# Log-softmax over 50,000 columns: the loads move from SyncE's queue to GpSimd's

## The chip, the cores and the metric

The kernel runs on one core of a Trainium2 chip. The core has five engines that run their own instruction streams and wait for one another through semaphores: TensorE (PE in the profile), VectorE (DVE), ScalarE (ACT), GpSimd (POOL) and SyncE (SP). Sixteen DMA engines move data between the chip's large memory (HBM) and the core's on-chip memory (SBUF, 128 partitions). A DMA is issued by an instruction of one of the engines. The metric is the device time of one execution in microseconds, the median of several runs.

## What is computed

For each of 16 x 512 = 8192 rows of 50,000 float32 values, the logarithm of the softmax:

```python
def reference(x: np.ndarray) -> np.ndarray:       # x: (16, 512, 50000)
    max_x = np.max(x, axis=-1, keepdims=True)
    shifted = x - max_x
    log_sum_exp = np.log(np.sum(np.exp(shifted), axis=-1, keepdims=True))
    return (shifted - log_sum_exp).astype(np.float32)
```

The input is 1638.4 MB, the output as much. Each value is read once and written once by the kernel.

## The kernel before

A tile is 32 rows, each cut in four quarters, so that 128 partitions hold 12,500 values each: 50,000 B per partition, 6.4 MB per tile, 256 tiles. Four buffers of that size fill SBUF. A tile lives in one buffer from its load to its store: it is loaded, reduced, exponentiated into a throw-away place for the sum, corrected in place, and stored from there.

Each engine has a part of its own; semaphores join them. `landed[j]` tells that the load into buffer j has landed, `stored[j]` that its store is done. A DMA adds 16 to its semaphore when it is complete. `take` waits for 16 and takes them off again, so that the same constant serves in each round.

```python
def take(engine, sem, n=16):
    engine.wait_ge(sem, n).then_inc(sem, -n)

@block.gpsimd
def _(gpsimd):
    view = ones.rearrange("p (r g) -> p r g", g=G)
    gpsimd.memset(ones, 1.0).then_inc(ready)
    # ... two affine_selects leave 1.0 where two partitions belong to one row

@block.sync
def _(sync):
    def load(j, src):
        sync.dma_start(out=bufs[j], in_=src).then_inc(landed[j], 16)

    for t in range(NBUF):
        load(t, xt[t])
    src = run(xt, NBUF, rounds)
    with sync.Fori(0, rounds) as q:           # 63 rounds of four tiles
        for j in range(NBUF):
            take(sync, stored[j])
            load(j, src(q, j))
    # ... then waits for the last stores
```

VectorE waits for the landing, takes the maxima of the four column pieces, spreads the row's maximum over its four partitions with two small transposes, and, once ScalarE and TensorE have made the logarithm of the sum, subtracts both in place:

```python
    def whole(j, by_pieces=False):
        take(vector, landed[j])
        for c in range(NS):                   # NS = 4 pieces of 3125 columns
            vector.tensor_reduce(
                out=negms[j][:, c : c + 1], in_=bufs[j][:, cols(c)],
                op=ALU.max, axis=AX, negate=True,
            ).then_inc(...)
        # ... negp, share(j), scaled
        subtract(j, ...)                      # tensor_scalar on the whole 128 x 12500 buffer

    with vector.Fori(0, rounds):
        for j in range(NBUF):
            whole(j)
        settle()
    for j in range(NBUF):
        whole(j, by_pieces=j == NBUF - 1)
```

ScalarE exponentiates piece by piece, with the sum as a by-product, and issues the stores. The store of a tile is issued in the midst of the next tile's work, ahead of its third piece (`GATE = 2`):

```python
        for c in range(NS):
            if c == GATE and dst is not None:
                store((j - 1) % NBUF, dst, bufs[(j - 1) % NBUF])
            shifted.next(scalar.activation(out=dump, in_=bufs[j][:, cols(c)], func=ACT.Exp, ...))
```

TensorE adds up the four partitions of a row with a matrix of ones (the one that GpSimd makes at the start).

Of the kernel before, what the change touches and what calls it, by code (L numbers as in the profile page):

```python
# [19 lines left out]
NBUF = 4  # L20

NS = 4
# [22 lines left out]
def take(engine, sem, n=16):  # L45

    engine.wait_ge(sem, n).then_inc(sem, -n)  # L47


def cols(c):  # L50
    return slice(c * C, (c + 1) * C)
# [3 lines left out]
def kernel(  # L55
# [14 lines left out]
    rounds = (ntiles - NBUF) // NBUF  # L70
    assert ntiles % NBUF == 0 and rounds >= 2

    xt = xf.rearrange("(t r) (g w) -> t (r g) w", r=R, g=G)
    ot = of.rearrange("(t r) (g w) -> t (r g) w", r=R, g=G)

    def run(a, first, n):

        part = a[first : first + NBUF * n].rearrange("(q i) p w -> q i p w", i=NBUF)
        return lambda q, i: part[bass.ds(q, 1), i].rearrange("o p w -> (o p) w")
# [13 lines left out]
    bufs = [data.tile([P, W], FP32, name=f"buf{j}") for j in range(NBUF)]  # L93
# [19 lines left out]
    def sem(name):  # L113
        return ctx.enter_context(nc.semaphore(name))

    landed = [sem(f"landed{j}") for j in range(NBUF)]
    stored = [sem(f"stored{j}") for j in range(NBUF)]
# [11 lines left out]
    block = ctx.enter_context(nc.Block())  # L129

    @block.gpsimd
    def _(gpsimd):
        view = ones.rearrange("p (r g) -> p r g", g=G)
        gpsimd.memset(ones, 1.0).then_inc(ready)  # L134
        gpsimd.affine_select(  # L135
            out=view, in_=view, pattern=[[-G, R], [0, G]], base=0,
            channel_multiplier=1, compare_op=ALU.is_ge, fill=0.0,
        ).wait_op(ready, 1, "sem-ge").then_inc(ready)
        gpsimd.affine_select(  # L139
            out=view, in_=view, pattern=[[G, R], [0, G]], base=G - 1,  # L140
            channel_multiplier=-1, compare_op=ALU.is_ge, fill=0.0,
        ).wait_op(ready, 2, "sem-ge").then_inc(ready)

    @block.sync
    def _(sync):
        def load(j, src):
            sync.dma_start(out=bufs[j], in_=src).then_inc(landed[j], 16)

        for t in range(NBUF):
            load(t, xt[t])  # L150
        src = run(xt, NBUF, rounds)
        with sync.Fori(0, rounds) as q:
            for j in range(NBUF):
                take(sync, stored[j])
                load(j, src(q, j))
        for j in range(NBUF - 1):
            take(sync, stored[j])
        take(sync, stored[NBUF - 1], 16 * NS)

    @block.vector  # L160
    def _(vector):
        def share(k):

            on_dve.next(
                vector.transpose(out=allneg, in_=negp.to_broadcast([P, SQ]))  # L165
            ).then_inc(on_dve.sem)
            on_dve.next(
                vector.tensor_reduce(  # L168
                    out=rowneg, in_=allneg.rearrange("p (r g) -> p r g", g=G),
                    op=ALU.min, axis=AX,  # L170
                )
            ).then_inc(on_dve.sem)
            on_dve.next(
                vector.tensor_copy(  # L174
                    out=spread.rearrange("p (r g) -> p r g", g=G),
                    in_=rowneg[:, :, None].to_broadcast([P, SQ // G, G]),
                )
            ).then_inc(on_dve.sem)
            on_dve.next(
                vector.transpose(out=negmaxs[k], in_=spread)  # L180
            ).then_inc(agreed.sem)

        def subtract(k, *bufs):
            for n, buf in enumerate(bufs):
                ins = vector.tensor_scalar(  # L185
                    out=buf, in0=buf, scalar1=negmaxs[k][:, 0:1], scalar2=logs[k],
                    op0=ALU.add, op1=ALU.subtract,
                )
                if n == 0:
                    logged.next(ins)  # L190
                ins.then_inc(subtracted.sem)

        def whole(j, by_pieces=False):
            take(vector, landed[j])

            for c in range(NS):
                vector.tensor_reduce(  # L197
                    out=negms[j][:, c : c + 1], in_=bufs[j][:, cols(c)],
                    op=ALU.max, axis=AX, negate=True,
                ).then_inc(shifted.sem if c < NS - 1 else on_dve.sem)  # L200
            on_dve.next(vector.nop()).then_inc(shifted.sem)  # L201
            vector.tensor_reduce(  # L202
                out=negp, in_=negms[j], op=ALU.min, axis=AX
            ).then_inc(on_dve.sem)
            share(j)

            rescaled.next(
                vector.tensor_mul(out=scaleds[j], in0=scales[j], in1=parts[j])  # L208
            ).then_inc(summed.sem)
            subtract(j, *([bufs[j][:, cols(c)] for c in range(NS)] if by_pieces else [bufs[j]]))  # L210

        def settle():
            for count in (on_dve, rescaled, logged):
                count.settle(vector)

        with vector.Fori(0, rounds):
            for j in range(NBUF):
                whole(j)
            settle()
        for j in range(NBUF):  # L220
            whole(j, by_pieces=j == NBUF - 1)

    @block.scalar
    def _(scalar):
# [97 lines left out]
```

## Time and profile before

| | before |
|---|---|
| time, median of 3 runs | 7589.62 us (7589.4 to 7590.59) |
| span of the profiled execution | 7588.4 us |
| tiles | 256, so 29.6 us each |
| VectorE waits for landings, in total | 923.3 us in 251 waits, the longest 18.9 |
| a load's issue on SyncE's queue | 333 ns median, 256 of them |
| a store's issue on ScalarE's queue | 339 ns median, 259 of them |
| first reduction on VectorE begins | 18.94 us |

The profile records one execution. Busy times say how much each engine worked; a row of 40 digits shows the busy share in tenths for 40 equal slices of the span; the waits say which engine sat idle for which other one. Moving data is no engine's busy time: it has a row of its own, with the mean busy share of the sixteen DMA engines and the bytes that they moved. An issue of a DMA is short; the time from issue to landing is listed apart. SPq, ACTq and DVEq stand for the engines' instruction queues, where waits and DMA issues are handled.

### The profile page before, as it was taken

How to read it: one execution, taken by the hardware profiler on the slowest of the kernel's cores; microseconds unless marked ns; L12 is line 12 of the kernel's file. 1: busy time of each engine (PE TensorE's matmuls, PEld its weight loads, DVE VectorE, ACT ScalarE, POOL GpSimd, SP SyncE). 2: the span in 40 equal slices, each digit the busy share in tenths (PEclk: the TensorE clock that was granted, in tenths of full speed). 3: DMA queues.
4: the chain of work that ended last, by engine and by line, in shares of the span. 5: the costliest groups of instructions: out<-in, count | busy, mean ns of one | idle time of the engine just before them, and what ended most of it. 6: DMA issues, size and time to landing. Idle time of an engine off the chain costs nothing. (4 is left out here: it accounts for less than half of the span.)

```text
span 7588.4 us, 13821 instructions
## 1 busy us (share of the span) xinstructions
PE 477.9 (6%) x2048; PEld 456.0 (6%) x2048; DVE 5440.6 (72%) x2819; ACT 3184.7 (42%) x2561; POOL 1.4 (0%) x7
## 2 busy tenths in 40 slices
PE   0000000000000000000000000000000000000000
PEld 0000000000000000000000000000000000000000
DVE  7767677777777777777777777777777777777776
ACT  4434444344443434444344443434444344444433
POOL 0000000000000000000000000000000000000000
DMA  9999999999999999999999999999999999999999
GB/s 417 432 432 433 434 431 434 434 433 433 434 433 431 434 434 433 431 434 433 432 434 434 431 434 434 432 433 434 434 431 434 434 434 432 434 434 431 434 434 400
DMA packets 74162, 3276.85 MB, mean 432 GB/s; under 512 B 8240, under 2 KB 8240, under 8 KB 8240
## 3 DMA queue, kind: packets, MB, share of 16 engines
q1 hardware_dynamic: 36864, 1638.42, 50.0%
q10 hardware_dynamic: 37296, 1638.42, 50.0%
q14 instruction: 2, 0.02, 0.0%
HBM read 1638.40 MB, written 1638.40 MB: 432 GB/s over the span
## 5 line engine op out<-in xcount | busy, mean ns | idle before, releaser
L239 ACT ACTIVATE dump<-buf,negm 128x3125 f32<-128x3125 f32 x1024 | 2937.3, 2868 | 3805.0 <-DVE negm L197 3765.7
L197 DVE TENSOR_REDUCE negm<-buf 128x1 f32<-128x3125 f32 x1024 | 3418.2, 3400 | 923.3 <-DVEq L47 923.3
L185 DVE TENSOR_SCALAR buf<-buf,negmax,logsum 128x12500 f32<-128x12500 f32 (+1 forms) x259 | 1738.9, 6715 | 553.8 <-ACT logsum L227 553.8
L277 PE MATMUL sums<-scaled,ones 128*128 128x1 f32 x2048 | 477.9, 355 | 7087.2 <-DVE scaled L208 7087.2
L277 PEld LDWEIGHTS sums<-scaled,ones 128*128 128x128 f32 x2048 | 456.0, 328 | 7109.0 <-DVE scaled L208 7109.0
L208 DVE TENSOR_TENSOR scaled<-scale,part 128x4 f32<-128x4 f32 x256 | 41.6, 163 | 580.4 <-ACT scale L247 580.4
L227 ACT ACTIVATE logsum<-sums 128x1 f32<-128x1 f32 x256 | 43.8, 171 | 551.0 <-PE sums L277 551.0
L239 ACT ACTIVATION_READ_ACCUMULATOR dump<-buf,negm 128x1 f32 x1024 | 190.8, 186 | 0.0
L247 ACT ACTIVATE scale<-negm,negmax 128x4 f32<-128x4 f32 x256 | 76.1, 297 | 23.6
L202 DVE TENSOR_REDUCE negp<-negm 128x1 f32<-128x4 f32 x256 | 40.1, 157 | 39.2 <-DVE negm L197 39.2
L180 DVE STREAM_TRANSPOSE negmax<-spread 128x32 f32<-128x32 f32 x256 | 54.2, 212 | 8.9
L165 DVE STREAM_TRANSPOSE allneg<-negp 128x32 f32<-128x32 f32 x256 | 54.1, 211 | 8.9
L168 DVE TENSOR_REDUCE rowneg<-allneg 128x8 f32<-128x32 f32 x256 | 47.6, 186 | 8.9
L174 DVE COPY spread<-rowneg 128x32 f32<-128x32 f32 x256 | 46.3, 181 | 8.9
L258 ACT ACT_TABLE_LOAD x1 | 1.3, 1283 | 1.0 <-SPq L111 1.0
L135 POOL TENSOR_SCALAR_AFFINE_SELECT ones<-ones 128x128 f32<-128x128 f32 x1 | 0.5, 519 | 0.1
L139 POOL TENSOR_SCALAR_AFFINE_SELECT ones<-ones 128x128 f32<-128x128 f32 x1 | 0.5, 519 | 0.1
L134 POOL MEMSET ones<- 128x128 f32 x1 | 0.2, 205 | 0.5 <-SPq L111 0.5
L306 POOL MEMSET const-bfloat16-1.0<- 128x1 bf16 x1 | 0.1, 103 | 0.0
L306 POOL MEMSET const-uint8-127<- 128x1 uint8 x1 | 0.1, 102 | 0.0
L306 POOL MEMSET const-float32-0.0<- 128x1 f32 x1 | 0.1, 99 | 0.3 <-issue 0.3
L306 POOL MEMSET const-float32-1.0<- 128x1 f32 x1 | 0.1, 99 | 0.0
## 6 DMA issues: line engine op xcount, KB each, us to landing
buf<-in_x_dram SPq DMA_DIRECT2D x256, 6250.0 KB, 36.7
out_dram<-buf ACTq DMA_DIRECT2D x255, 6250.0 KB, 41.6
out_dram<-buf ACTq DMA_DIRECT2D x4, 1562.5 KB, 11.3
```

Of the source, the lines that this page charges most:

```text
L165: vector.transpose(out=allneg, in_=negp.to_broadcast([P, SQ]))
L168: vector.tensor_reduce(out=rowneg, in_=allneg.rearrange("p (r g) -> p r g", g=G), op=ALU.min, axis=AX,)
L174: vector.tensor_copy(out=spread.rearrange("p (r g) -> p r g", g=G), in_=rowneg[:, :, None].to_broadcast([P, SQ // G, G]),)
L180: vector.transpose(out=negmaxs[k], in_=spread)
L185: ins = vector.tensor_scalar(out=buf, in0=buf, scalar1=negmaxs[k][:, 0:1], scalar2=logs[k], op0=ALU.add, op1=ALU.subtract,)
L197: vector.tensor_reduce(out=negms[j][:, c : c + 1], in_=bufs[j][:, cols(c)], op=ALU.max, axis=AX, negate=True,).then_inc(shifted.sem if c < ...
L202: vector.tensor_reduce(out=negp, in_=negms[j], op=ALU.min, axis=AX).then_inc(on_dve.sem)
L208: vector.tensor_mul(out=scaleds[j], in0=scales[j], in1=parts[j])
L227: scalar.activation(out=logs[k], in_=rowsums[k], func=ACT.Ln)
L239: scalar.activation(out=dump, in_=bufs[j][:, cols(c)], func=ACT.Exp, bias=negms[j][:, c : c + 1], scale=1.0, accum_out=parts[j][:, c : c + 1],
L247: scalar.activation(out=scales[j], in_=negms[j], func=ACT.Exp, bias=negmaxs[j][:, 0:1], scale=-1.0,)
L277: ins = tensor.matmul(rowsums[j], ones, scaleds[j][:, c : c + 1], start=c == 0, stop=c == NS - 1,)
```

## The change

The loads are issued by GpSimd instead of SyncE. A DMA issued by SyncE or ScalarE has its descriptors (the records that tell a DMA engine what to move) made by hardware; one issued by GpSimd has them made by software on that engine. SyncE is left with nothing to do. GpSimd first issues the four loads of the start, then makes the matrix of ones, then goes through the loop of waits and loads.

VectorE no longer takes 16 off `landed[j]` after each landing. The count grows: in round q it waits for 16(q + 1), a value that is computed from the loop's counter into a register once a round, and for the last four tiles for a constant.

```diff
@@ GpSimd and SyncE @@
     @block.gpsimd
     def _(gpsimd):
         view = ones.rearrange("p (r g) -> p r g", g=G)
+
+        def load(j, src):
+            gpsimd.dma_start(out=bufs[j], in_=src).then_inc(landed[j], 16)
+
+        for t in range(NBUF):
+            load(t, xt[t])
         gpsimd.memset(ones, 1.0).then_inc(ready)
 # ... (the two affine_selects as they were)
-
-    @block.sync
-    def _(sync):
-        def load(j, src):
-            sync.dma_start(out=bufs[j], in_=src).then_inc(landed[j], 16)
-
-        for t in range(NBUF):
-            load(t, xt[t])
         src = run(xt, NBUF, rounds)
-        with sync.Fori(0, rounds) as q:
+        with gpsimd.Fori(0, rounds) as q:
             for j in range(NBUF):
-                take(sync, stored[j])
+                take(gpsimd, stored[j])
                 load(j, src(q, j))
         for j in range(NBUF - 1):
-            take(sync, stored[j])
-        take(sync, stored[NBUF - 1], 16 * NS)
+            take(gpsimd, stored[j])
+        take(gpsimd, stored[NBUF - 1], 16 * NS)
@@ VectorE @@
-        def whole(j, by_pieces=False):
-            take(vector, landed[j])
+        def whole(j, nth, by_pieces=False):
+            vector.wait_ge(landed[j], nth)
 # ...
-        with vector.Fori(0, rounds):
+        with vector.Fori(0, rounds) as q:
+            nth = vector.snap(q * 16 + 16)
             for j in range(NBUF):
-                whole(j)
+                whole(j, nth)
             settle()
         for j in range(NBUF):
-            whole(j, by_pieces=j == NBUF - 1)
+            whole(j, 16 * (rounds + 1), by_pieces=j == NBUF - 1)
```

The order of the computing instructions on VectorE, ScalarE and TensorE is the same as before.

## The prediction

> **What bounds the kernel now.** I read the page first: its shares of busy time, its DMA row in 40 slices, and its list of DMA issues.
>
> ```profile
> span 7588.4 us, 13821 instructions
> PE 477.9 (6%) x2048; PEld 456.0 (6%) x2048; DVE 5440.6 (72%) x2819; ACT 3184.7 (42%) x2561; POOL 1.4 (0%) x7
> ...
> DMA  9999999999999999999999999999999999999999
> ...
> HBM read 1638.40 MB, written 1638.40 MB: 432 GB/s over the span
> ...
> buf<-in_x_dram SPq DMA_DIRECT2D x256, 6250.0 KB, 36.7
> out_dram<-buf ACTq DMA_DIRECT2D x255, 6250.0 KB, 41.6
> ```
>
> No compute engine is near full; the DMA engines are, in every slice. The stretches in windows say whether that is really a ceiling (the last two columns are the DMA share and GB/s):
>
> ```profile
> 500.00:1000.00 500.00, 29.87 (x128) 28.50 (x128) 356.58 (x186) 209.12 (x167) 0.00 (x0) 1.00 1.00 433
> 2000.00:4000.00 2000.00, 126.94 (x544) 121.12 (x544) 1435.73 (x747) 839.62 (x676) 0.00 (x0) 1.00 1.00 433
> 7530.00:7590.00 60.00, 3.74 (x16) 3.56 (x16) 29.75 (x22) 15.90 (x14) 0.00 (x0) 1.00 0.75 319
> ```
>
> In the middle the share is 1.00 at a flat 433 GB/s. All 3276.8 MB at 433 GB/s take 7568 us; only some 20 us of 7588 are start and tail, most of it in the last 60 us, where the share is 0.75. So the time is bytes over rate, and only four things can move it: the rate, gaps in which both DMA queues are empty, the start, the tail.
>
> Next, how far each queue is from running empty. The timeline of two tiles in the middle:
>
> ```profile
> 3004.72 0.34 ACTq L231 DMA_DIRECT2D out_dram<-buf  x1
> ...
> 3013.98 6.79 DVE L185 TENSOR_SCALAR buf<-buf,negmax,logsum 128x12500 f32<-128x12500 f32 x1 [2.16 <-ACT logsum L227]
> 3017.01 29.84 SPq L147 DMA_DIRECT2D buf<-in_x_dram  x2
> 3024.32 13.35 DVE L197 TENSOR_REDUCE negm<-buf 128x1 f32<-128x3125 f32 x4 [3.55 <-DVEq L47]
> ...
> 3034.24 0.34 ACTq L231 DMA_DIRECT2D out_dram<-buf  x1
> ...
> 3043.50 6.79 DVE L185 TENSOR_SCALAR buf<-buf,negmax,logsum 128x12500 f32<-128x12500 f32 x1 [2.16 <-ACT logsum L227]
> 3053.82 13.35 DVE L197 TENSOR_REDUCE negm<-buf 128x1 f32<-128x3125 f32 x4 [3.53 <-DVEq L47]
> ```
>
> One tile takes 3053.82 - 3024.32 = 29.5 us, which is 12.8 MB (6.4 in, 6.4 out) at 433 GB/s. VectorE works 26.0 of it and idles 3.5 before the landing. A load takes 36.7 us from issue to landing while loads are finished every 29.5, so when a load is issued there are still 7.2 us of the load before it in the queue. For stores it is 41.6 - 29.5 = 12.1 us. Neither queue runs empty, and when one does, the other has work. That one direction alone fills the engines is seen at the start: the first three loads, issued at 1.0, about 1.4 and 2.0 us with nothing else moving, landed 17.8, 32.1 and 46.4 us after issue, 14 to 15 us apart, and 6.4 MB at 433 GB/s are 14.8 us.
>
> **What the Trainium skill says.** "DMA: Bandwidth & Descriptors", section "Where 436 GB/s comes from", puts the ceiling of 16 engines at 435 GB/s; the trace's 433 is 99.5% of that, so no way of issuing can win much more than half a percent. The same page, "Queues, rings and completion order": each DMA engine goes round the queues with work, one packet at a time, and a packet can be several descriptors. The page of before counts 36864 packets for 256 loads, 144 each: 128 rows of 50,000 B and 16 ends, so loads and stores now share row by row; how software-made descriptors are grouped no run here shows yet. The same page, "Latency and other measured facts": first byte after about 1 us for the software path against about 0.6 for the hardware one; no run here shows it. "SBUF — State Buffer", section "SBUF: two separate sides": while VectorE runs an operation in a 2-port mode, GpSimd is locked out of the shared port pair and cannot write descriptors, so the DMA engines starve. Of the subtraction (12500 elements in 6.79 us, 1.84 per ns, where the reduction does 3125 in 3.40, 0.92 per ns) the trace gives the double rate that such a mode would have. GpSimd issues nothing in the kernel before, so its trace cannot confirm the lock.
>
> **The change part by part.**
>
> 1. *The issuer.* 256 loads move from SyncE's queue to GpSimd. In the trace SyncE issues 3.03 us into the 6.79 us subtraction (3017.01 against 3013.98), so with the lock a software-made load would start 3.76 us later; at worst 6.79. Add about 1 us for the writing of descriptors (my estimate, above the 0.4 us that the skill's two latencies differ by). Delay d: about 5 us, at worst 8. Against it stand 7.2 us of load backlog: at 5 us nothing is seen; at 8 us the load queue is empty for 0.8 us, in which the stores, with 12.1 us of backlog, take the whole rate and give their buffers back sooner. Cost in the loop: 252 loads x 0 = 0.
>
> 2. *VectorE's wait.* 256 times a wait followed by a subtraction from the semaphore becomes a wait against a register (63 rounds of four) or a constant (the last four); one multiply-add of the loop counter is added per round, 63 in all. Even at 0.1 us each (an estimate; the trace has register operations on SyncE's queue at 37 ns, 0.06 at most) it lies in the 3.5 us that VectorE idles before the landing. Cost: 0.
>
> 3. *GpSimd's own work.* The memset and two selections that make the ones matrix now come after four load issues. TensorE needs them at 36.02 us; they took 1.4 us from 1.02 on. Even with several us for each issue this is in time. Cost: 0.
>
> 4. *Start.* The first load was issued at 1.03 us and landed 17.8 us later. GpSimd can begin at about the same moment (its memset started at 1.02), but descriptors take longer: +1 to +3 us, all of it on the path, since nothing is in flight yet.
>
> 5. *Tail.* The last load landed at about 7546 us, then 26 us of compute and the quartered stores. If queues share as before, unchanged: 0. If loads come in larger packets and are favoured, the last tiles land sooner and the 0.25 x 60 = 15 us of idle DMA are partly filled: up to -9 us. I give this a third: -3.
>
> Rate: unchanged, as the same 50,000 B rows move; for possible fetches of descriptors from memory I add +0.03%, 2 us. Sum: 2 + 2 - 3 = +1, and the skew to the slow side makes it 7592 us.
>
> **The rivals.**
>
> *Starvation counts in full.* If each load's 3.76 us behind the subtraction, and 1 us of writing, were idle time of the DMA engines, 252 x 4.8 = 1200 us would be added: 8800 us. For it: the issue does fall in the subtraction. Against it: the two backlogs, and VectorE's chain of 26.0 us with room for 3.5. It would need both queues empty at once, or a generation far longer than 8 us. At a generation of about 20 us (backlogs of 7.2 + 12.1 used up) the loop would begin to stretch.
>
> *The rate falls.* If descriptors in memory slow the loads by 4%, half the traffic, the whole is 2% slower: 7740 us. A single slow DMA engine would do it too, as every transfer is spread over all 16. For it: all the time is rate, nothing would hide it. Against it: one descriptor stands for 50,000 B, 1.85 us of an engine at 27 GB/s, ample time to fetch the next.
>
> *Loads are favoured.* Large packets would let a load pass in 15 to 20 us rather than 36.7, and stores would wait longer. VectorE would idle less before landings and more before buffers. The bytes stay the same; only the tail gains: about 7580 us.
>
> *VectorE is held up.* If GpSimd has the port when the subtraction wants to start, the tile's 26.0 us grow by a us or two, still under 29.5: no change.
>
> **Range and chances.** The kernel is at a rate that nothing in the change touches, and both new delays fall into waits that are there already. Start +1 to +3, tail -9 to 0, rate -0.2 to +0.6%, -15 to +45 us: 7570 to 7640 holds it 8 times in 10. Faster by 2% would need 7438 us, 441 GB/s over the whole span: hardly possible, 0.02. Slower by 2% needs the rate to fall or a generation of some 20 us: 0.08. Within 2%: 0.90.
>
> **What will show it.** Right: the stretch 2000 to 4000 us still has DMA share 1.00 and 432 to 433 GB/s; VectorE's wait for landings stays near 923 us in total; the loads of the queue on GpSimd are issued within some us of the store's landing. A start 1 to 3 us later in the first reduction (18.94 us before). The lock, if it exists, shows as issues that end just after a subtraction, without loss. The rival of starvation would show DMA shares under 0.95 and VectorE waiting 4 us more per tile; the rate rival, share 1.00 at fewer GB/s; the favoured loads, a time from issue to landing well under 36.7 us and a longer one for stores. What would make me wrong: software descriptors that cut the 50,000 B rows into small pieces, or an issue that takes tens of us.

## The result: 110 us slower, and the profile after

| | before | after |
|---|---|---|
| time, median | 7589.74 us (7589.4 to 7590.59, 4 runs) | 7698.5 us (7671.28 to 7704.14, 4 runs) |
| ratio | 1 | 1.0136, 95% interval 1.012 to 1.0152 |
| VectorE waits for landings, in total | 923.3 us | 1033.6 us |
| a load's issue, mean | 0.33 us | 3.33 us |

The change costs 1.4%. The predicted 7592 us and its range of 7570 to 7640 were too low; of the three chances, "within 2%" with 0.90 is what happened.

Two lines of the page of before that the prediction does not show, the loads' queue and VectorE's wait for landings (busy, mean ns | idle before, releaser):

```profile
q1 hardware_dynamic: 36864, 1638.42, 50.0%
...
L197 DVE TENSOR_REDUCE negm<-buf 128x1 f32<-128x3125 f32 x1024 | 3418.2, 3400 | 923.3 <-DVEq L47 923.3
```

The page of the changed kernel, cut to the lines that answer to those of before: busy time, the rows in 40 slices, the DMA queues, two groups (busy, mean ns | idle before, releaser) and the DMA issues (median us to landing):

```profile
span 7699.4 us, 13628 instructions
PE 477.9 (6%) x2048; PEld 456.0 (6%) x2048; DVE 5441.5 (71%) x2819; ACT 3184.7 (41%) x2561; POOL 852.8 (11%) x263
...
POOL 0111111021101211110111111121100000000000
DMA  9999999999999999999999999999999999999999
...
q0 software_dynamic: 36864, 1638.42, 50.3%
q10 hardware_dynamic: 37296, 1638.42, 49.6%
...
HBM read 1638.40 MB, written 1638.40 MB: 426 GB/s over the span
...
L195 DVE TENSOR_REDUCE negm<-buf 128x1 f32<-128x3125 f32 x1024 | 3418.3, 3400 | 1033.6 <-DMA buf<-in_x_dram 1033.6
...
L136 POOL DMA_DIRECT2D buf<-in_x_dram x256 | 851.4, 3326 | 6760.4 <-POOLq L47 6702.2
...
buf<-in_x_dram POOLq DMA_DIRECT2D x256, 6250.0 KB, 41.0
out_dram<-buf ACTq DMA_DIRECT2D x255, 6250.0 KB, 38.4
```

The bytes, the packets of the load queue (36864) and the engines' work are what they were. VectorE waits 1033.6 - 923.3 = 110.3 us longer for landings, and the span is 111.0 us longer (7699.4 - 7588.4): the whole loss shows as later landings. GpSimd is busy 851.4 us with issuing. A load takes 41.0 us from issue to landing (36.7 before), a store 38.4 (41.6 before).

The windows of the changed kernel, in the columns of before's (the last two are DMA share and GB/s):

```profile
2000.00:4000.00 2000.00, 123.22 (x528) 117.56 (x528) 1418.32 (x731) 829.13 (x665) 271.01 (x66) 1.00 1.00 426
4000.00:6000.00 2000.00, 125.06 (x536) 119.32 (x536) 1406.65 (x734) 824.74 (x666) 293.45 (x67) 1.00 1.00 425
6000.00:7500.00 1500.00, 93.35 (x400) 89.06 (x400) 1064.90 (x551) 621.77 (x500) 32.14 (x50) 1.00 1.00 427
...
7640.00:7700.00 60.00, 3.73 (x16) 3.56 (x16) 30.57 (x22) 16.62 (x16) 0.00 (x0) 1.00 0.74 317
```

The DMA share is still 1.00, the rate 425 to 427 GB/s where it was 433. Start and tail have hardly moved (the last 60 us: share 0.74, 317 GB/s; before 0.75, 319). Taken by itself, "share 1.00 at fewer GB/s" looks like slower transfers, and I had named it as the sign of that. The experiments below do not bear that out for software-made descriptors.

The timeline of two tiles of the changed kernel (start, duration, then the instruction; in brackets the idle time before and its releaser):

```profile
3006.81 0.34 ACTq L230 DMA_DIRECT2D out_dram<-buf  x1
...
3016.08 6.79 DVE L183 TENSOR_SCALAR buf<-buf,negmax,logsum 128x12500 f32<-128x12500 f32 x1 [2.16 <-ACT logsum L226]
3016.18 6.80 POOL L136 DMA_DIRECT2D buf<-in_x_dram  x1 [23.24 <-POOLq L47]
3026.93 13.35 DVE L195 TENSOR_REDUCE negm<-buf 128x1 f32<-128x3125 f32 x4 [4.06 <-DMA buf<-in_x_dram]
...
3036.85 0.34 ACTq L230 DMA_DIRECT2D out_dram<-buf  x1
...
3046.02 7.00 POOL L136 DMA_DIRECT2D buf<-in_x_dram  x1 [23.03 <-POOLq L47]
3046.11 6.79 DVE L183 TENSOR_SCALAR buf<-buf,negmax,logsum 128x12500 f32<-128x12500 f32 x1 [2.16 <-ACT logsum L226]
...
3056.85 13.35 DVE L195 TENSOR_REDUCE negm<-buf 128x1 f32<-128x3125 f32 x4 [3.95 <-DMA buf<-in_x_dram]
```

Both issues shown begin within 0.1 us of the start of a subtraction and end with it, the first at 3016.18 + 6.80 = 3022.98 against 3016.08 + 6.79 = 3022.87. This is the lock that the Trainium skill describes ("SBUF — State Buffer", section "SBUF: two separate sides": whichever of VectorE's two-port operation and GpSimd's operation comes first keeps the shared ports for its whole instruction). The holding agrees with it; the order does not settle it, since the second issue is held although it begins 0.09 us before its subtraction (3046.02 against 3046.11). Over the run the issues fall into two kinds: 134 of 256 take about 0.53 us, the other 122 more than 2 us, the longest 7.017, and these end within 0.13 us of a subtraction's end.

Held issues are not the whole of it, as this same run shows. In the window from 6000 to 7500 us one of 50 issues is held (GpSimd is busy for 32.14 us in all), in the two windows before it 40 of 66 and 45 of 67 are; the rate is 427 GB/s there, against 426 and 425. The loss goes on when the holding has stopped.

A tile now takes 3056.85 - 3026.93 = 29.9 us, 0.4 more than before.

### The profile page after: what moved, and what is told of

Its sections match the earlier page's. It is cut to its first block, busy times and chain, and to the rows that moved or that the text cites. A ratio compares the mean times of both kernels' runs of the same rounds, so it can differ in the third digit from the quotient of the medians.

```text
span 7699.4 us, 13628 instructions
## 1 busy us (share of the span) xinstructions
PE 477.9 (6%) x2048; PEld 456.0 (6%) x2048; DVE 5441.5 (71%) x2819; ACT 3184.7 (41%) x2561; POOL 852.8 (11%) x263
## 3 DMA queue, kind: packets, MB, share of 16 engines
q0 software_dynamic: 36864, 1638.42, 50.3%
## 5 line engine op out<-in xcount | busy, mean ns | idle before, releaser
L195 DVE TENSOR_REDUCE negm<-buf 128x1 f32<-128x3125 f32 x1024 | 3418.3, 3400 | 1033.6 <-DMA buf<-in_x_dram 1033.6
L183 DVE TENSOR_SCALAR buf<-buf,negmax,logsum 128x12500 f32<-128x12500 f32 (+1 forms) x259 | 1739.5, 6717 | 553.8 <-ACT logsum L226 553.8
L136 POOL DMA_DIRECT2D buf<-in_x_dram x256 | 851.4, 3326 | 6760.4 <-POOLq L47 6702.2
L206 DVE TENSOR_TENSOR scaled<-scale,part 128x4 f32<-128x4 f32 x256 | 41.6, 163 | 579.8 <-ACT scale L246 579.8
## 6 DMA issues: line engine op xcount, KB each, us to landing
out_dram<-buf ACTq DMA_DIRECT2D x255, 6250.0 KB, 38.4
```

What stands on the lines that cost most here:

```text
L136: gpsimd.dma_start(out=bufs[j], in_=src).then_inc(landed[j], 16)
L183: ins = vector.tensor_scalar(out=buf, in0=buf, scalar1=negmaxs[k][:, 0:1], scalar2=logs[k], op0=ALU.add, op1=ALU.subtract,)
L195: vector.tensor_reduce(out=negms[j][:, c : c + 1], in_=bufs[j][:, cols(c)], op=ALU.max, axis=AX, negate=True,).then_inc(shifted.sem if c < ...
```

## Where the slack really was

The prediction set a delay of some 5 us against 7.2 us of backlog of the loads and 12.1 us of the stores. The kernel before can be asked directly. These are the two DMA queues of before in six windows of 2 us each, starting at 3018, 3022, 3028, 3034, 3036 and 3042 us (packets that begin in it, MB, time of these packets as a share of 16 engines; q1 are the loads, q10 the stores):

```profile
q10 hardware_dynamic: 16, 0.80, 92.7%
q1 hardware_dynamic: 1, 0.00, 0.0%
...
q1 hardware_dynamic: 13, 0.60, 69.4%
q10 hardware_dynamic: 5, 0.25, 28.9%
...
q1 hardware_dynamic: 18, 0.90, 104.1%
...
q1 hardware_dynamic: 15, 0.75, 86.7%
q10 hardware_dynamic: 2, 0.05, 5.8%
...
q10 hardware_dynamic: 11, 0.55, 63.6%
q1 hardware_dynamic: 15, 0.25, 29.2%
...
q10 hardware_dynamic: 16, 0.80, 92.6%
```

Loads and stores do not share row by row on most engines: nearly all together, they do a whole load and then a whole store. The load issued at 3017.01 (timeline in the prediction) is taken up by most engines between 3022 and 3024, when they have just finished a store. The store issued at 3034.24 has 63.6% of the time in 3036 to 3038, when the engines have just finished a load. So most engines have nothing else to do when the next transfer comes, and the slack is some 5 us for a load and some 3 us for a store.

The trace's packet records, put together into 16 series by end and next start (the records don't name the engine), show how 36.7 us from issue to landing goes with so little slack. Each engine carries 8 rows of 50,000 B of a tile, 1.847 us each. A load has landed when its last engine is done, and the engines are not in step. Of the load issued at 3017.01, ten engines end their part at 3037.0 to 3037.3, four by 3040.7, one at 3047.8 and the last at 3053.4, some 16 us after the first. The 7.2 us are the backlog of that last engine, which does have rows of both queues in turn.

The same records show where the 110 us lie. The excess of each row's time over 1.847 us, added up over the run and divided by 16 engines:

```
                           span      excess in loads   in stores   sum (us per engine)
before                   7588.4            10.5            6.0        16.5
after                    7699.4            91.0           30.4       121.4
stores one piece later   7829.3            73.8          159.9       233.6
no large subtraction     7643.3            25.0           45.7        70.7
subtraction in pieces    7611.8            17.9           17.3        35.2
```

After minus before is 105 of the 111 us of span. A longer span has to show in long rows or in gaps, since the rows are the same in number; the table says that it is rows (the gaps grew by some 6 us). Two thirds of the excess after is in the first or last rows of a transfer, and two thirds in rows of 1.9 to 2.6 us instead of 1.85. I read this as engines that run dry: the waiting lies inside the time of a packet record, and the DMA share stays at 1.00. The records do not show the waiting itself.

And the reading is not complete. It fits the engines that lead. The ones that lag have rows of both queues to do; if they lost nothing they would catch up. In the changed kernel two engines are 13.6 us behind the first at 1.0 ms and 18 behind at 7.5 ms, so they lose as much per tile as the rest. What slows them is not shown. (The other three lines belong to experiments below: the third to a run with GATE 3.)

## The experiments

My theory: late issue. Most engines, I supposed, run dry between two transfers, for a fraction of a us, 256 times. Rivals: the software-made descriptors are slower to carry; the register wait costs; the port lock is all of it; the loss is something else that belongs to GpSimd.

### The wait alone

The kernel before with VectorE's growing count only:

```diff
-            take(vector, landed[j])
+            vector.wait_ge(landed[j], nth)
```

> SyncE still issues all loads with hardware descriptors; only VectorE's wait is the growing one. The theory of slow rings (software-made descriptors make the loads slower on a few of the 16 DMA engines, and the slowest paces all) and the theory of late issue (the subtraction holds back GpSimd by up to 7 us, more than the real slack) both expect 7590 us, 433 GB/s in the middle. The theory of the wait (the register wait on VectorE costs the 110 us) expects 7700.

7589.85 us, ratio 1.0 (0.9991 to 1.0008). The wait costs nothing; the loss is in the issuing.

### Loads alone, from either engine

These two leave out everything but the loads: the reductions, exponentials, subtraction and 252 of the 256 stores. The issuing engine waits for a buffer's landing and loads it again.

```diff
-                take(sync, stored[j])
+                eng.wait_ge(landed[j], nth)      # eng: sync, or gpsimd
                 load(j, src(q, j))
```

> Only the loads of all 256 tiles, issued by SyncE, each after the landing of the load before it in the same buffer; no compute, and of the stores only the last four buffers (the output is left out but for those). At the 433 GB/s of one direction: 3784 us of loads and about 60 of stores and start, 3840 to 3860. Control for the next run.

> The same with GpSimd issuing. Nothing on VectorE, so no port is held; three loads are always queued, so no issue is late. Slow rings: 1.5 to 3% longer than the control, 3900 to 3960 us. Late issue (or anything in the loop of loads and stores): within 0.3% of the control.

SyncE 3853.09 us (3852.92 to 3853.27), GpSimd 3853.97 (3853.70 to 3854.24). From the page of the GpSimd one:

```profile
buf<-in_x_dram POOLq DMA_DIRECT2D x256, 6250.0 KB, 58.5
```

and a window of it (columns: POOL, clock, share, GB/s):

```profile
1000.00:3000.00 2000.00, 71.21 (x135) 1.00 1.00 433
```

433 GB/s, and 0.9 us difference in the whole time, the size of the later start. As long as three further loads are queued, software-made descriptors carry as fast as hardware-made ones. That answers the rate rival for loads alone; for a loop with stores, a stretch at 434 GB/s under GpSimd, at the end of this section, speaks against it.

### Half of the loads

Buffers 0 and 2 loaded by GpSimd, 1 and 3 by SyncE.

```diff
-            for j in range(NBUF):
+            for j in range(0, NBUF, 2):          # the odd ones: SyncE, as before
                 take(gpsimd, stored[j])
                 load(j, src(q, j))
```

> GpSimd loads two of the four buffers, SyncE the other two. Slow rings: half the loss, about 7645 us (7625 to 7665). Late issue: every second load is late, which still empties the queue each second tile: anything from 7620 to 7700, not separated from slow rings by this run alone.

7652.25 us (7643.03 to 7662.75), ratio 1.0085 (1.0068 to 1.0102): some 57% of the loss for half of the loads, as late issue, the lock and slower descriptors alike would have it.

### Without the subtraction, and with the subtraction in four pieces

The first leaves out the subtraction of all columns but one, so there is nothing long for an issue to be held by. The second does all the work, in four instructions.

```diff
@@ no_sub @@
-                    out=buf, in0=buf,
+                    out=buf[:, 0:1], in0=buf[:, 0:1],
@@ split_sub @@
-            subtract(j, *([bufs[j][:, cols(c)] for c in range(NS)] if by_pieces else [bufs[j]]))
+            subtract(j, *[bufs[j][:, cols(c)] for c in range(NS)])
```

> The changed kernel with the subtraction cut to one column of 12500, so that VectorE holds no port for long (the output lacks the subtraction on the other columns). Issues on GpSimd should all take about 0.5 us. Late issue: back to 7585 to 7600 us. Slow rings: still 7670 to 7710 us, 425 to 427 GB/s in the middle.

> The changed kernel with the subtraction in four pieces of 1.9 us, so that GpSimd can come in between two of them. Late issue: issues of at most about 2.5 us in place of 7, and a time between the run without subtraction and the changed kernel, 7640 to 7680 us. If the length of the hold does not matter: 7690 to 7710.

Without it: 7648.57 us, ratio 1.0072 (1.0055 to 1.0089); the issues take 0.53 us. In pieces: 7624.15 us, ratio 1.0048 (1.0031 to 1.0066). In the trace of the second:

```profile
L136 POOL DMA_DIRECT2D buf<-in_x_dram x256: 527/1892/2135, 1.7 to 7527.6; - x128
```

An issue is now held for one piece of the subtraction, 1.9 us (minimum, median and maximum in ns), not for four. So taking the long hold away is worth 50 to 74 of the 109 us. It isn't all: the first expectation, 7585 to 7600 without the lock, was missed by about 50 us. The second was missed too, to the good side (7624 against 7640 to 7680). Nor does the loss follow the lateness: from the end of a store to the end of the next load's issue it is 0.87 us in the mean before, 1.6 without the subtraction and 2.9 with it in pieces, and the run with the longer lateness loses less.

Without the subtraction the loss sets in late, with no change in the instructions:

```profile
500.00:1000.00 500.00, 31.72 (x136) 30.26 (x136) 250.50 (x187) 211.39 (x170) 8.97 (x17) 1.00 1.00 434
2000.00:4000.00 2000.00, 125.00 (x536) 119.27 (x536) 987.50 (x738) 833.29 (x671) 35.36 (x67) 1.00 1.00 429
```

The engines ended a load within 6 us of one another at 1.0 ms, and two were 15 to 17 us behind at 2.1 ms. A lag of 16 us alone costs nothing, as before shows.

### Lateness under hardware descriptors: through a small memset, an empty instruction, twenty memsets

Loads stay with SyncE, but GpSimd passes the landing of the store on.

```diff
@@ GpSimd, new; SyncE waits for go[j] @@
+                take(gpsimd, stored[j])
+                gpsimd.memset(scratch[j], 0.0).then_inc(go[j])    # hw_locked, 128 x 32
+                gpsimd.nop().then_inc(go[j])                      # hop_only, in its place
+                # hw_late: twenty memsets of 128 x 128 in a row, in its place
```

> Before, but after each store's landing GpSimd first does a small memset and only then lets SyncE issue the load. The memset should be held up by the subtraction as the software-made load is (5 to 7 us where it falls into it). Late issue: 7670 to 7710 us, 425 to 427 GB/s. Slow rings: 7585 to 7600 us, 432 to 433 GB/s, although the issue is as late.

> The kernel before, in which GpSimd takes the signal that a store has landed and hands it on to SyncE with an empty instruction; SyncE issues the loads with descriptors made by hardware. Nothing for the port lock to hold up; the issue comes some 0.1 to 0.3 us later. If so small a lateness by itself puts the loop over its edge, as the run with the small memset (7653 us) seems to say: 7630 to 7680 us. If there it was the memset that now and then fell into the subtraction: 7585 to 7600 us.

> Before, with hardware descriptors, but between a store's landing and the next load's issue GpSimd makes 20 small memsets in a row (about 5 us, more where the subtraction holds them up). Slow rings being out by the loads-only pair, the question is whether lateness alone makes the whole loss. Late issue: 7670 to 7720 us, 425 to 428 GB/s. If software-made descriptors still have a share of their own in a loop with stores: clearly under 7670.

| | time, us | ratio (interval) |
|---|---|---|
| empty instruction | 7589.5 | 1.0 (0.9991 to 1.0009) |
| one small memset | 7653.28 (7634.89 to 7705.84) | 1.0107 (1.007 to 1.0144) |
| twenty memsets | 8186.11 (8173.57 to 8195.71) | 1.0784 (1.0769 to 1.0799) |

The run with twenty memsets was to be late by the 5 us or so that they take when nothing holds them; it was late by over 11, because they too were held by the subtraction, and it cost far more than the 7670 to 7720 us expected. Its timeline shows it:

```profile
3027.19 0.20 POOL L149 MEMSET scratch<- 128x128 f32 x1 [20.60 <-POOLq L47]
3027.45 11.05 POOL L151 MEMSET scratch<- 128x128 f32 x18
```

So does the group of the middle eighteen on its page (busy, mean ns):

```profile
L151 POOL MEMSET scratch<- 128x128 f32 x4536 | 2485.8, 548 | 261.5
```

And a window of it:

```profile
2000.00:4000.00 2000.00, 116.45 (x500) 111.06 (x499) 1325.93 (x683) 771.14 (x621) 659.71 (x1247) 1.00 0.98 399
```

Hardware-made descriptors issued 11 us late cost about 596 us, 2.4 us for each of 252 loads. Lateness of the load is enough to lose time, without a software-made descriptor. Here, at 399 GB/s, the share has at last begun to fall, to 0.98.

The small memset is the odd one: 7653 us lies in neither of the ranges expected. It was to be late only when held, but all its memsets take 124 ns except two within the first 200 us, the longest of them 6452, as the view of that tile shows (minimum, median, maximum in ns):

```profile
L148 POOL MEMSET scratch<- x252: 124/124/6452, 78.8 to 7551.6; 128x32 f32 x126
```

Two windows of it:

```profile
2000.00:4000.00 2000.00, 126.95 (x544) 121.13 (x544) 1431.09 (x743) 836.21 (x674) 8.44 (x68) 1.00 1.00 432
5000.00:7000.00 2000.00, 125.06 (x536) 119.32 (x536) 1420.64 (x737) 830.10 (x669) 8.31 (x67) 1.00 1.00 428
```

It goes at 432 GB/s until past 4 ms (by the page's row of slices), and at 428 afterwards, with no change in the instructions. The records show three engines that have fallen 17 to 18 us behind by then, where there had been a spread of 2 to 3 us. The empty instruction, which leaves out the memset's 0.12 us and its writing, stays at 433. What tips the run with the memset is not settled.

### The store earlier or later, hardware descriptors

`GATE` places the store's issue in ScalarE's work; one step is a piece, 3.3 us (from 1 to 0 it is 10 us, since that store need not wait for the next landing). Nothing else is changed, and GpSimd has no part in it.

```diff
-GATE = 2
+GATE = 3      # gate3_sp; 1: gate1_sp; 0: gate0_sp
```

> The kernel before with the store of a tile issued ahead of the first piece of the next tile, not the third, so that it no longer waits for the next landing and is 13 us earlier. The queues get more slack. Both theories: 7580 to 7595 us; it cannot gain much as the rate is at its ceiling.

> The kernel before with each store issued one piece of ScalarE's work earlier (GATE 1). Late issue: a load queue that has slack gains nothing by more of it, 7580 to 7592 us, the same as before.

> The kernel before, its loads on SyncE's queue as they were, with one constant changed: each store is issued one piece of ScalarE's work later (GATE 3 in place of 2, about 3.3 us). Late issue, whoever issues: the loop from the landing of a tile over its store to the next load has no slack left at GATE 2, so 3.3 us more cost as much as GpSimd's lateness does, 7640 to 7750 us, with a DMA share of 1.00 at 425 to 430 GB/s. If the loss belongs to GpSimd's issuing alone: 7585 to 7600 us at 433 GB/s.

| GATE | time, us | ratio (interval) |
|---|---|---|
| 0 | 7588.07 (7573.18 to 7612.16) | 0.9999 (0.999 to 1.0007) |
| 1 | 7588.14 (7584.24 to 7591.68) | 0.9997 (0.9989 to 1.0006) |
| 2 (before, run beside 1 and 3) | 7590.15 (7586.02 to 7592.11) | 1 |
| 3 | 7739.38 (7670.65 to 7831.02) | 1.0167 (1.0113 to 1.022) |

Earlier gains nothing; later by one piece costs as much as the whole change, or more; its 3.3 us are just more than the slack of some 3 us that the windows of before show for a store. A window of the kernel with GATE 3 (the profile is of the longest of its runs, which the ratio leaves out):

```profile
2000.00:4000.00 2000.00, 122.72 (x527) 117.08 (x527) 1394.35 (x718) 811.22 (x652) 0.00 (x0) 1.00 1.00 420
```

And its DMA issues on the page:

```profile
buf<-in_x_dram SPq DMA_DIRECT2D x256, 6250.0 KB, 37.9
out_dram<-buf ACTq DMA_DIRECT2D x255, 6250.0 KB, 40.3
```

It is the changed kernel's signature, share 1.00 at a lower rate, without one software-made descriptor. The table of row excess above adds the direction: make loads late, and the long rows are the loads' (91.0 of 121.4 us); make stores late, and they are the stores' (159.9 of 233.6). The run without the subtraction does not fit: there it is loads that come late, and 45.7 of 70.7 us are in stores. The tuned kernel sat at the last gate that costs nothing.

### The changed kernel with earlier stores

> The changed kernel with that earlier store. Late issue (the loop of landings, compute, stores and loads has no slack left when GpSimd issues): back to 7585 to 7610 us. Slow rings: 7660 to 7710 us, since the slowest DMA engine paces all whatever the slack.

> The changed kernel with the store one piece earlier (ahead of the second, 3.3 us earlier). Late issue: each us of slack counts, so between 7600 and 7698, about 7640 to 7670.

> The changed kernel with both cures together: the subtraction in four pieces, and each store issued ahead of the first piece of the next tile's exponentials (GATE 0). Late issue: neither lock nor lateness reaches the loop, 7585 to 7600 us at 433 to 434 GB/s. If something of the issue by GpSimd stays that neither touches: 7610 to 7640 us.

> The same late issue with the store issued ahead of the next tile's first piece (13 us earlier). Late issue: 7585 to 7615 us, as the earlier store gives back the slack. If the memsets slow something by themselves: still 7670 or more.

```diff
-GATE = 2
+GATE = 0      # gate0_pool; 1: gate1_pool; 0 and the subtraction in pieces: split_gate0
```

| | time, us | ratio (interval) |
|---|---|---|
| GpSimd, GATE 1 | 7609.4 (7600.86 to 7640.45) | 1.0032 (1.0014 to 1.0051) |
| GpSimd, GATE 0 | 7599.92 (7588.5 to 7643.08) | 1.0023 (1.0013 to 1.0032) |
| GpSimd, GATE 0, subtraction in pieces | 7627.66 (7587.44 to 7656.32) | 1.0043 (1.0025 to 1.0061) |
| SyncE behind twenty memsets, GATE 0 | 7648.37 (7623.47 to 7697.75) | 1.0084 (1.005 to 1.0119) |

The page of GATE 0 on GpSimd, the group of its issues and the times from issue to landing:

```profile
L136 POOL DMA_DIRECT2D buf<-in_x_dram x256 | 135.2, 528 | 7371.0 <-POOLq L47 7306.1
...
buf<-in_x_dram POOLq DMA_DIRECT2D x256, 6250.0 KB, 47.4
out_dram<-buf ACTq DMA_DIRECT2D x255, 6250.0 KB, 44.2
```

A window of the same kernel:

```profile
2000.00:4000.00 2000.00, 126.92 (x544) 121.09 (x544) 1434.01 (x746) 836.67 (x675) 35.46 (x68) 1.00 1.00 434
```

One constant gives back about nine tenths of the loss (98.6 of 108.8 us). It acts in two ways at once: the loads' issues no longer fall into the subtraction (528 ns in the mean, none held), and both queues now have a backlog. The loads' time beyond the 29.5 us of a tile has grown to 47.4 - 29.5 = 17.9 us, and the stores' is 14.7. And now the engines do share, as its queues in two windows of 2 us, from 3034 and 3036, show (q0 loads, q10 stores):

```profile
q0 software_dynamic: 11, 0.55, 63.5%
q10 hardware_dynamic: 7, 0.35, 40.4%
...
q10 hardware_dynamic: 9, 0.45, 51.9%
q0 software_dynamic: 8, 0.40, 46.2%
```

The first line came out better than the 7640 to 7670 us expected. The last two are misses. With lock and lateness both taken care of I expected 7585 to 7600 and got a spread from 7587 to 7656. In the trace of the third line (split_gate0) the excess is 70.8 us, 68.5 of it in loads, and mostly in their early rows (1.9 to 2.6 us), although the engines here do alternate between a store's and a load's rows. The twenty memsets at GATE 0 were not held (205 ns each), so the load came some 5 us later after its store than at GATE 0 alone and, as the store is issued 13.4 us earlier than at GATE 2, still ahead of where that has it; the run went at 433 GB/s from 2000 to 4000 us and at 413 from 6000 to 7500. Like the one with the small memset it holds for 4 ms and then slides.

So a remainder of 10 to 60 us is neither the lock nor plain lateness: under SyncE the loads of GATE 1 and 2 come later than these and cost nothing. Their issues end 22.6 and 22.5 us (median) after the first reduction of the tile two before; those of GATE 1 and 0 under GpSimd 15.3 and 12.3 us after it, those without the subtraction 19.7. What its cases have in common is that GpSimd writes something (descriptors or a memset) ahead of each load; where it only passes a signal on, nothing is lost. That is a pattern and no proof. A constant delay of about 1 us ahead of SyncE's loads, without GpSimd, would have tested it; it wasn't run.

No version beats the kernel before: GATE 0 and 1 under SyncE have the lowest medians, 7588.1 us, and both intervals include 1.

## Why the prediction was wrong

**What bounds it: half right.** Bytes over rate, share 1.00, VectorE with room: all still so in the changed kernel. But that the DMA engines are full "in every slice" was read from a share that does not tell these runs apart. It is 1.00 at 433, at 426 and at 420 GB/s.

**The failed step: part 1, "Against it stand 7.2 us of load backlog ... Cost in the loop: 252 loads x 0 = 0".** The delay itself was well sized: predicted about 5 us, at worst 8. Measured, a load that isn't held starts 0.6 us later (from the first issue to the first reduction: 20.16 - 1.67 = 18.49 us, before 18.94 - 1.03 = 17.91), and the mean issue adds 3.33 - 0.53 = 2.8 us, so 3.4 in the mean, about 7 at worst. What was wrong is what stood against it. "Neither queue runs empty, and when one does, the other has work" holds for the engines that lag. The others do a load, then a store, then a load, with some 5 us of slack for the load, where 7.2 had been set. A held load is beyond that. An unheld one is not, and yet the changed kernel without the subtraction, which has no held load, still loses 58 us; so the lost slack is shown as the step that failed, and only part of its price is explained. The measured cost is 109/252 = 0.43 us per load. The sentence behind it, "loads and stores now share row by row", was an inference from 144 packets per load; the two-microsecond windows of before's own trace refute it.

**The lock: right as a mechanism.** Issues do end with the subtraction. "Without loss" was wrong: without the long hold 50 to 74 us come back.

**VectorE's wait: 0, right** (7589.85 us alone). **GpSimd's own work: 0, right**: the ones matrix is ready by 5.3 us, far ahead of 36.02.

**Start: right.** The first reduction begins at 20.16 us, 1.2 later; I had given 1 to 3, all of it for descriptors. About half (0.64) is that GpSimd's first issue begins later. **Tail: -3 was wrong**, it is unchanged; the load queue's packets number 36864 as before, and loads were not favoured.

**The rivals.** Starvation in full (8800 us) was far off in size, and its sign, a DMA share under 0.95, did not show; yet late loads do cost time: about an eighth of the delay comes through (0.43 of 3.4 us), and at 11 us of lateness a fifth (2.4 us per load). The rate rival had the nearest number (7740) and the announced sign, and is not borne out in its cause: loads alone run at 433 GB/s from GpSimd. VectorE is not held up (its subtractions take 1739.5 us in all, 1738.9 before).

**What stays open.** Why 35 to 60 us remain at GATE 2 with the lock gone, and 10 to 40 at GATE 0; why the changed kernel goes on losing after 6 ms, when issues are no longer held; what slows the engines that lag; why splitting the subtraction does at least as well as leaving it out; why engines fall out of step, and why a loop that has run for 4 ms without loss then loses.

## What to carry to other kernels

Before you set a delay against a backlog, look at the queues in windows much shorter than a tile: issue-to-landing time was the slowest engine's here, and said nothing of the slack of the others. A DMA share of 1.00 does not prove a ceiling; GB/s against the best stretch does. Where loads must be issued by GpSimd, issue the stores that free their buffers as early as the dependence allows (here that gave back 98.6 of 108.8 us), and keep the issue of loads out of VectorE operations that hold it, such as this subtraction.

## What the runs showed of the hardware

- Time lost by the DMA engines stands in long packets (rows of 1.9 to 2.6 us and some longer, where 1.847 is usual) and hardly in gaps: share 1.00 at 426 GB/s, and at 420.
- GpSimd's issue of a 6.4 MB load takes 0.53 us, and up to 7.017 when VectorE's subtraction has the shared ports. GpSimd's memset is held in the same way (124 ns, once 6452; of twenty in a row the middle eighteen 548 ns each in the mean, where 205 is usual).
- "DMA: Bandwidth & Descriptors", section "Latency and other measured facts", has the software path's first byte about 0.4 us later than the hardware one's; the difference in the first landing here is 0.6 us. The section also reports that two of the engines are usually slower, with traffic to the software descriptors' rings as its guess. With loads alone no such cost appeared: 3853.97 us against 3853.09.
- In loops of loads and stores sixteen DMA engines that start in step drift apart, in the kernel before within about a millisecond, until one or a few carry rows some 16 us behind the rest, and a transfer has then landed only when the last of them is done. With loads alone they stay within some 1 us of one another.
